# Four gate tiles of the last embedding as Strassen block products

## The chip, the cores and the metric

One Trainium2 chip, one core. The kernel is one launch that runs on that core's engines: TensorE (PE; its weight loads are shown apart as PEld), VectorE (DVE), ScalarE (ACT), GpSimd (POOL) and SyncE (SP, which only issues transfers). The metric is the device time of one execution in microseconds. Before the change it is 1931.98 us, the median of three runs (1931.47 to 1932.03).

## The reference

One inference step of a two-layer decoder: 512 prompt rows and 8 x 4 sample rows, together T = 544 tokens, width 1024. Each layer is a half-weighted SwiGLU, a mixer (a chunked spatial-gating unit in layer 0, forgetting attention in layer 1), a second half-weighted SwiGLU, and a gated embedding of the layer's own input `pe`. What matters here is the end of layer 1:

```python
h = h + 0.5 * swiglu(rmsnorm(h, ffn2_norm[i]), ffn2_w1[i], ffn2_w3[i], ffn2_w2[i])
gate = jax.nn.sigmoid(rmsnorm(h, ple_norm[i]) @ ple_w_gate[i])   # (544, 1024) @ (1024, 1024)
h = h + gate * (pe[i] @ ple_w_proj[i])                            # (544, 256) @ (256, 1024)
```

After layer 1 that `h` is the output y. All arrays are float32.

## The kernel before

**Layout.** The residual `h` lies transposed in SBUF: eight chunks of 128 features, each a row of 544 tokens per partition. A product of two float32 arrays is made from pairs: each operand is split into a rounded half `hi` and a rest `lo` (ACT casts, DVE subtracts: `split_pair` L329/L330 for activations, `_split` L241/L242 for weights, `prep` L341/L342 for a chunk of `h` times its norm's gain), and PE adds hi x hi, hi x lo and lo x hi. A matmul has 128 x 128 weights and 272 of the 544 tokens (HT). A tile of 128 outputs over 1024 features therefore takes 8 x 3 x 2 = 48 matmuls (`mm`, lines L285, L289 and L291 for the three parts). The norm's factor is a number per token, `rstd`; it isn't needed before the product, and multiplies the result.

**Weights.** A list of pieces, in the order of use, is loaded (L208), for some pieces added or subtracted (`_sum`, L227), and split, so many pieces ahead of the product as `ahead` says: (splits, sums, loads), (2, 2, 4) in general and (2, 3, 6) around Strassen products.

**Strassen products.** The wide products of the feed-forward networks (FFN) are made in blocks: 256 features by 256 outputs, against two chunks by two halves of the tokens. Instead of eight block products there are seven (SEVEN = "1562734"), each over sums or differences of blocks. The sums of weight blocks are the pieces with `sum` (`seven`); those of the activations are made by `forms`: for a pair of chunks two ACT copies (L351), three DVE differences (L355, L357, L358) and two splits. One product is 4 x 3 x 2 = 24 matmuls (L538), and adds into one of three PSUM accumulators: A and C are PSUM tiles of the group `ps` (three tiles, rotating), B two tiles of the group `pb`. Behind a step its result is copied or added (L546, L553, L555, L557, L560). A gate then follows in the FFN: times `rstd` (L496), an activation (L499), and so on.

**The last FFN's tail.** The second FFN product is made in parts; its last part runs over chunks 0 to 7 of `h`. Chunk c's PSUM tile is read by `update` (L577), which adds to h[c], and `on_chunk` follows: `prep` for the next norm, and its sum of squares (ACT L368, POOL L370). `next_norm` can also make `forms` behind a chunk (`early`); for the last embedding it makes none. The steps of an FFN stand in a block for which PE, ACT, DVE and POOL keep the order in which the code issues them. Elsewhere a planner orders each engine's instructions, by its own estimate of when each becomes ready.

**The last embedding.** `ple` with layer 1: eight gate tiles by `tile_mm`, each times `rstd` (L765) and through a sigmoid (L766); behind the first two the pieces with w_proj are taken. From the third tile on, a product with `pe` (12 matmuls) follows two tiles behind, is multiplied by the gate (L776), and added to h (L777); then h[n] is stored by SP. Behind gate tile 6 come products 4, 5 and 6, and `ple_last` makes tile 7 in two halves of the tokens, so that the first half's gate, addition and store (L735 to L742) run beside the second half.

Of the kernel before, what the change touches and what calls it, by code (L numbers as in the profile page):

```python
# [36 lines left out]
T = SEQ + NS  # L37
HT = T // 2
# [13 lines left out]
NKP = NC_ // 2  # L52
# [3 lines left out]
SEVEN = "1562734"  # L56
# [16 lines left out]
G_FFN1, G_MIX, G_FFN2, G_PLE = 0, 16, 32, 48  # L73
# [10 lines left out]
COLS = ((0, HT), (HT, T))  # L84
# [3 lines left out]
def woven(x):  # L88

    return x.rearrange("p (a b) -> p b a", a=2)  # L90


def turns(out):

    return out.rearrange("p (b a) -> p b a", a=2)


def unwoven(out):

# [28 lines left out]
def span(p):  # L128

    return p[:].rearrange("p a b -> p (a b)")[:, 512 - HT:512 - HT + T]  # L130


def whole(p):

    return unwoven(span(p))


class Builder:
# [207 lines left out]
    def forms(self, h, gcol, n, xs):  # L346

        nc = self.nc
        x = self.big()
        for a in range(2):  # L350
            nc.scalar.activation(x[:, a, :], h[2 * n + a], AF.Copy, scale=self.gain(gcol + 2 * n + a))  # L351
        t13, t24 = self.tmp(), self.tmp()
        two = lambda t: t.rearrange("p (a b) -> p a b", a=2)
        f13, f24 = self.big(F32R), self.big(F32R)
        nc.vector.tensor_tensor(two(t13), x[:, :, HT:], two(x[:, 0, :]), ALU.subtract)  # L355
        self.split_pair(f13, t13)
        nc.vector.tensor_tensor(t24[:, :HT], x[:, 1, HT:], t13[:, :HT], ALU.subtract)  # L357
        nc.vector.tensor_tensor(t24[:, HT:], x[:, 1, :HT], t24[:, :HT], ALU.subtract)  # L358
        self.split_pair(f24, t24)
        half = lambda t, b: tuple(x[:, b * HT:(b + 1) * HT] for x in t)  # L360
        f13, f24 = ((t[:, 0, :], t[:, 1, :]) for t in (f13, f24))
        return {"1": half(xs[2 * n], 0), "2": half(xs[2 * n + 1], 0), "3": half(xs[2 * n + 1], 1),
                "5": half(f13, 0), "7": half(f13, 1), "6": half(f24, 0), "4": half(f24, 1)}
    def ssq(self, acc, h, cols=slice(0, T), first=False):

        nc = self.nc
        sq = acc[:, cols] if first else self.tmp()[:, cols]
        nc.scalar.activation(sq, h[:, cols], AF.Square)  # L368
        if not first:
            nc.gpsimd.tensor_tensor(acc[:, cols], acc[:, cols], sq, ALU.add)  # L370
# [120 lines left out]
    def gate(self, hid, rstd, j, a, g):  # L491

        nc, tt = self.nc, self.nc.vector.tensor_tensor

        def one():
            tt(g, g, rstd.unsqueeze(1).broadcast_to([P, 2, T]), ALU.mult)  # L496

        def two():
            nc.scalar.activation(g[:, 0], g[:, 0], AF.Silu)  # L499

        def three():
            tt(g[:, 1], g[:, 1], g[:, 0], ALU.mult)  # L502

        def four():
            pair = self.big(F32R)
            self.split_pair(pair, g[:, 1])
            hid[j, a] = pair[:, 0, :], pair[:, 1, :]
        return [one, two, three, four]
# [215 lines left out]
                    if k == n == a == 0:  # L724
                        self.tc.keep_in_program_order(i)

    def ple_last(self, h, gates, rstd, xs, wp, pp, y):

        nc, tt = self.nc, self.nc.vector.tensor_tensor
        c = NC_ - 1  # L730
        a = self.tmp()
        outs = [self.pb(), self.pb()]
        self.cols_mm(outs, self.blocks(self.unit()), xs)
        for (u, v), out in zip(COLS, outs):
            tt(halves(a[:, u:v]), unwoven(out[:, :v - u]), halves(rstd[:, u:v]), ALU.mult)  # L735
            nc.scalar.activation(a[:, u:v], a[:, u:v], AF.Sigmoid)
        outs = [self.ps()[:, 0, :], self.ps()[:, 0, :]]
        self.cols_mm(outs, wp[2 * c:2 * c + 2], pp)
        for (u, v), out in zip(COLS, outs):
            tt(halves(a[:, u:v]), unwoven(out[:, :v - u]), halves(a[:, u:v]), ALU.mult)  # L740
            tt(h[c][:, u:v], h[c][:, u:v], a[:, u:v], ALU.add)
            nc.sync.dma_start(out=y[c][:, u:v], in_=h[c][:, u:v])  # L742

    def ple(self, h, box, layer, on_chunk):
        nc = self.nc
        xs = self.pairs(box)
        pp = []
        for c in range(2):
            raw = self.tmp()
            nc.sync.dma_start(out=raw, in_=self.i["pe"][layer, c])  # L750
            pair = self.big(F32R)
            self.split_pair(pair, raw)
            pp.append((pair[:, 0, :], pair[:, 1, :]))
        rstd, gates, wp = None, [], []
        last = layer == 1
        for c in range(NC_ + 2):
            if c < NC_:
                if rstd is None:
                    p1, rstd = self.tile_rstd(xs, box["acc"])
                else:  # L760
                    p1 = self.tile_mm(xs)

                def gate(p1=p1):
                    a = self.tmp()
                    nc.vector.tensor_tensor(halves(a), whole(p1), halves(rstd), ALU.mult)  # L765
                    nc.scalar.activation(a, a, AF.Sigmoid)  # L766
                    gates.append(a)
                self.evac(gate)
            if c < 2:
                hi, lo = self.unit()  # L770
                wp += [(hi[:, P * k:P * k + P], lo[:, P * k:P * k + P]) for k in range(8)]
            for n in (range(c - 2, c + 1) if last and c == NC_ - 2 else [c - 2] if c >= 2 else ()):
                p2 = self.ps()
                self.mm(p2, wp[2 * n:2 * n + 2], pp, True, True)
                a = gates[n]
                nc.vector.tensor_tensor(halves(a), whole(p2), halves(a), ALU.mult)  # L776
                nc.vector.tensor_tensor(h[n], h[n], a, ALU.add)  # L777
                on_chunk(n)
            if last and c == NC_ - 2:
                self.ple_last(h, gates, rstd, xs, wp, pp, self.o["y"])  # L780
                return


    def square(self, raw):
        sq = self.tmp()
# [584 lines left out]
    def build(self):  # L1370
        nc, i, o = self.nc, self.i, self.o
# [4 lines left out]
                self.add_plain(ap)  # L1376

        def ple_units(n):
            for c in range(NC_):
                self.add_plain(i["wg"][n, c])  # L1380
                if c < 2:
                    self.add_plain(i["wp"][n, c])
# [10 lines left out]
        plain([i["woh"][k, c] for k in range(2) for c in range(NC_ // 2)] + [i["wo"][c] for c in range(NC_)])  # L1393
        self.ffn_pieces(3)
        ple_units(1)

        self.eps = self.const.tile([P, 1], F32, name="eps")
        nc.vector.memset(self.eps, EPS)
# [5 lines left out]
        t = self.pb()  # L1404
# [5 lines left out]
        h = [self.hp[c // 2][:, c % 2, :] for c in range(NC_)]  # L1410
# [15 lines left out]
        box = {"x": {}, "f": [], "acc": self.st()}  # L1426
# [35 lines left out]
        box = nxt  # L1462
        box, rstd = self.kv(h, box, G_FFN1 + 8)
        on, nxt = self.next_norm(h, G_MIX + 8)
        self.ffn(h, box, G_FFN1 + 8, rstd, on)
        box = nxt
        on, nxt = self.next_norm(h, G_FFN2 + 8, early={5: 0, 6: 1})
        self.attention(self.pairs(box), box["acc"], h, on)
        box = nxt
        on, nxt = self.next_norm(h, G_PLE + 8)  # L1470
        self.ffn(h, box, G_FFN2 + 8, None, on)
        box = nxt
        self.ple(h, box, 1, lambda c: nc.sync.dma_start(out=o["y"][c], in_=h[c]))


def _stationary(w):

    k, m = w.shape
    return np.ascontiguousarray(
        w.reshape(k // P, P, m // P, P).transpose(2, 1, 0, 3).reshape(m // P, P, k // P * P))  # L1480


def _blocks(w):

    k, m = w.shape
    return w.reshape(k // 256, 2, P, m // 256, 2, P).transpose(3, 4, 1, 2, 0, 5).reshape(m // 256, 4, P, k // 256, P)


def _constants():
# [30 lines left out]
def _arrays(x_prompt, x_sample, p_prompt, p_sample, cache_k, cache_v, cache_logf, page_table, ffn1_norm, ffn1_w1,  # L1520
# [16 lines left out]
    a["w13q"] = np.stack([_stationary(w[0][:, 256:512]) for w in (ffn1_w1, ffn1_w3)])  # L1537
    a["w13p"], a["w13"], a["w2a"], a["w2b"] = (np.stack(x) for x in (w13p, w13, w2a, w2b))
    a["wg"] = np.stack([_stationary(w) for w in ple_w_gate])
    a["wp"] = np.stack([_stationary(w).reshape(2, 4, P, 2 * P).transpose(0, 2, 1, 3).reshape(2, P, 8 * P)  # L1540
                        for w in ple_w_proj])
    a["win"], a["wout"] = _stationary(gmlp_w_in[0]), _stationary(gmlp_w_out[0])
# [53 lines left out]
```

## Time and profile before

| | |
|---|---|
| median of three runs | 1931.98 us |
| profiled execution, its own time | 1931.48 us |
| its span, first to last instruction | 1929.7 us |
| granted TensorE clock | 1.0 |
| PE busy | 1906.5 us (99%), 16508 matmuls |
| DVE busy | 1457.5 us (76%) |
| ACT busy | 950.2 us (49%) |
| POOL busy | 142.6 us (7%) |
| first gate tile of the last embedding starts | about 1869.6 us |
| DVE ends | 1926.94 us |

A row of the groups reads: line, engine, operation, output <- inputs by the program's names, shapes, count | busy us, mean ns of one | idle time before, with what released it. A row of the timeline reads: start and length in us, engine, line and so on; in brackets is how long the engine was idle before it and for whom. Successive matmuls overlap in the records, so the length of one is not their spacing. A row of the waits gives the waiting instruction, the one it waited for, and the total, the count and the longest.

### The profile page before, as it was taken

To read this page: it belongs to the slowest core of one execution; us is meant where nothing else is said; L and a number is where in the kernel's file an instruction comes from. 1 tells how busy PE (TensorE), PEld (TensorE's weight loads), DVE (VectorE), ACT (ScalarE), POOL (GpSimd) and SP (SyncE) were. 2 spreads that over 40 slices of the span, in tenths; PEclk is the share of its full clock that TensorE was granted. 3 is DMA by queue.
4 is the path that set the end of the run, shared out by engine and by line. 5 is a ranking of instruction groups with operands and counts; after the bars stand their busy time and mean duration, and the time that the engine had idled before them with its cause. 6 is when DMAs were issued, how large, how long until landed. Compare 5 with 4: busy or idle time off the path is not lost.

```text
span 1929.7 us, 39007 instructions
## 1 busy us (share of the span) xinstructions
PE 1906.5 (99%) x16508; PEld 1872.2 (97%) x16508; DVE 1457.5 (76%) x1799; ACT 950.2 (49%) x1396; POOL 142.6 (7%) x190
## 2 busy tenths in 40 slices
PE   9999999999999999999999999999999999999999
PEld 8999999999999999999999999999977899999999
DVE  7887877556788877766578887877476888878774
ACT  7544434424554444454466454444374754444461
POOL 0000000410100000023000000001131300000020
PEclk9999999999999999999999999999999999999999
DMA  5233234312223233431484232324769332332431
GB/s 195 79 112 121 84 123 147 108 48 88 88 88 107 86 120 105 153 104 45 144 306 157 103 129 69 129 86 136 217 210 341 101 110 81 112 113 86 139 109 47
DMA packets 98048, 237.62 MB, mean 123 GB/s; under 512 B 12130, under 2 KB 29826, under 8 KB 97874
## 3 DMA queue, kind: packets, MB, share of 16 engines
q1 hardware_dynamic: 97730, 235.09, 36.9%
q8 instruction: 130, 2.13, 0.5%
q14 instruction: 44, 0.36, 0.1%
q10 hardware_dynamic: 144, 0.04, 0.0%
HBM read 218.65 MB, written 16.44 MB: 122 GB/s over the span
## 4 chain that ended last, share of the span: by engine, by line
PE 89%; DVE 6%; ACT 3%; issue 1%; DMA 1%; POOL 0%; SPq 0%; ACTq 0%; DVEq 0%; POOLq 0%
PE ps L538 31%; PE ps L285 15%; PE ps L291 15%; PE ps L289 15%; PE pb L538 5%; DVE big L242 2%; ACT big L241 1%; DVE big L227 1%; DMA big<-in_cv 1%; PE ps L891 1%; PE ps L892 1%; PE ps L893 1%; DVE big L496 0%; DVE big L330 0%; PE ps L1285 0%
## 5 line engine op out<-in xcount | busy, mean ns | idle before, releaser
L538 PE MATMUL ps<-big,big 128*128 128x272 f32 x5616 | 668.8, 279 | 5.9 <-DVE big L555 3.5
L538 PEld LDWEIGHTS ps<-big,big 128*128 128x128 f32 x5616 | 658.5, 189 | 7.0 <-issue 4.0
L242 DVE TENSOR_TENSOR big<-big,big 128x1024 fp32r<-128x1024 f32 (+2 forms) x505 | 582.8, 1157 | 93.4 <-ACT big L241 92.9
L241 ACT CAST big<-big 128x1024 fp32r<-128x1024 f32 (+2 forms) x505 | 483.1, 977 | 326.5 <-DVE big L227 251.9
L285 PE MATMUL ps<-big,big 128*128 128x272 f32 x2668 | 531.3, 280 | 3.8 <-ACT big L241 2.3
L291 PE MATMUL ps<-big,big 128*128 128x272 f32 x2668 | 529.2, 280 | 1.8 <-DVE big L242 1.7
L289 PE MATMUL ps<-big,big 128*128 128x272 f32 x2668 | 528.3, 279 | 0.0
L285 PEld LDWEIGHTS ps<-big,big 128*128 128x128 f32 x2668 | 408.3, 189 | 8.5 <-ACT big L241 5.7
L291 PEld LDWEIGHTS ps<-big,big 128*128 128x128 f32 x2668 | 407.9, 189 | 3.6 <-DVE big L242 3.1
L289 PEld LDWEIGHTS ps<-big,big 128*128 128x128 f32 x2668 | 407.9, 189 | 0.0
L370 POOL TENSOR_TENSOR st<-st,tmp 128x544 f32<-128x544 f32 (+1 forms) x63 | 87.5, 1389 | 1476.7 <-ACT tmp L368 1476.5
L227 DVE TENSOR_TENSOR big<-big,big 128x1024 f32<-128x1024 f32 x156 | 190.2, 1219 | 0.0
L577 DVE SCALAR_TENSOR_TENSOR big<-ps,big 128x544 f32<-128x544 f32 x128 | 92.5, 723 | 104.0 <-PE ps L291 103.0
L546 ACT COPY tmp<-ps 128x544 f32<-128x544 f32 x117 | 71.6, 612 | 107.5 <-PE ps L538 107.2
L496 DVE TENSOR_TENSOR big<-big,st 128x1088 f32<-128x1088 f32 x88 | 113.2, 1289 | 3.3 <-ACT big L560 2.0
L538 PE MATMUL pb<-big,big 128*128 128x272 f32 x936 | 114.8, 279 | 0.0
L538 PEld LDWEIGHTS pb<-big,big 128*128 128x128 f32 x936 | 111.3, 189 | 0.0
L499 ACT ACTIVATE big<-big 128x544 f32<-128x544 f32 x88 | 58.0, 660 | 88.1 <-DVE big L496 88.0
L341 ACT ACTIVATE big<-big,gains 128x544 fp32r<-128x544 f32 (+1 forms) x80 | 55.3, 703 | 90.3 <-DVE big L577 55.0
L330 DVE TENSOR_TENSOR big<-big,big 128x544 fp32r<-128x544 f32 (+1 forms) x112 | 79.4, 715 | 22.8 <-ACT big L329 22.6
L342 DVE SCALAR_TENSOR_TENSOR big<-big,gains,big 128x544 fp32r<-128x544 f32 (+1 forms) x80 | 64.6, 817 | 23.4 <-ACT big L341 23.4
L329 ACT CAST big<-big 128x544 fp32r<-128x544 f32 (+1 forms) x112 | 71.2, 644 | 11.9 <-DVE big L502 7.5
(218 smaller groups left out, 1388.5 us busy)
## 6 DMA issues: line engine op xcount, KB each, us to landing
big<-in_w SPq DMA_DIRECT2D x156, 512.0 KB
big<-in_w2b SPq DMA_DIRECT2D x96, 384.0 KB
big<-in_w13p SPq DMA_DIRECT2D x16, 512.0 KB
big<-in_w2a SPq DMA_DIRECT2D x16, 512.0 KB
big<-in_win SPq DMA_DIRECT2D x16, 512.0 KB
big<-in_wg SPq DMA_DIRECT2D x16, 512.0 KB
big<-in_ck SPq DMA_DIRECT2D x16, 512.0 KB
big<-in_cv SPq DMA_DIRECT2D x16, 512.0 KB
```

Source lines behind the costliest of these rows:

```text
L227: self.nc.vector.tensor_tensor(t, a, b, ALU.add if op == "+" else ALU.subtract)
L241: self.nc.scalar.copy(hi, src)
L242: self.nc.vector.tensor_tensor(lo, src, hi.bitcast(F32), ALU.subtract)
L285: i = nc.tensor.matmul(o, wh, xh[:, b], start=s, stop=False)
L289: nc.tensor.matmul(o, wh, xl[:, b], start=False, stop=False)
L291: nc.tensor.matmul(o, wl, xh[:, b], start=False, stop=e)
L330: self.nc.vector.tensor_tensor(pair[:, 1, cols], src, pair[:, 0, cols].bitcast(F32), ALU.subtract)
L370: nc.gpsimd.tensor_tensor(acc[:, cols], acc[:, cols], sq, ALU.add)
L496: tt(g, g, rstd.unsqueeze(1).broadcast_to([P, 2, T]), ALU.mult)
L538: nc.tensor.matmul(turns(dst[w]), a[:, c], woven(b), start=k in "152" and kp == 0 and n == 0, stop=kp == NKP - 1 and n == 2, skip_group_ch ...
L546: nc.scalar.copy(t["r" + k], t["C" if k == "5" else "A"])
L577: nc.vector.scalar_tensor_tensor(halves(h[c]), whole(out), 0.5, halves(h[c]), ALU.mult, ALU.add)
```

## The change

Gate tiles 0 to 3 stay as they are. Gate tiles 4 to 7 of layer 1 become seven block products with a new weight array `wg7`, which holds the same weights in blocks. Forms of chunk pairs 0 and 1 are made behind chunks 1 and 3 of the last FFN, those of pairs 2 and 3 behind gate tiles 2 and 3. The order on PE is: gate tiles 0 to 3, products 0 to 3, seven steps, products 4, 6 and 5, and product 7 in two halves. The gates of tiles 4 and 6 come from step "3", those of 5 and 7 from step "4" (each pair is one 1088-wide multiplication by `rstd` and one sigmoid). The additions to h of tiles 4, 6 and 5 run on GpSimd. Reading `pe` becomes a function of its own, with the same instructions.

```diff
+    def strassen(self, xf, done):
+        nc, tt, t = self.nc, self.nc.vector.tensor_tensor, {}
...
+        def step(k):
+            hi, lo = self.unit()
+            self.advance()
+            if k == "2":
+                t["B"] = [self.pb()[:, :HT] for _ in range(2)]
+            elif k in "15":
+                t["A" if k == "1" else "C"] = self.ps()[:, :, :HT]
+            out = t["A" if k in "1674" else "C" if k in "53" else "B"]
+            for kp in range(NKP):
+                xh, xl = xf[kp][k]
+                for n, (a, b) in enumerate(((hi, xh), (hi, xl), (lo, xh))):
+                    for w in range(2):
+                        c = slice(512 * w + P * kp, 512 * w + P * kp + P)
+                        nc.tensor.matmul(turns(out[w] if k == "2" else out[:, w]), a[:, c], woven(b),
...
+            if k in "156":
+                t["r" + k] = self.tmp().rearrange("p (w b) -> p w b", w=2)
+                nc.scalar.copy(t["r" + k], out)
+            elif k == "2":
+                t["g"] = self.big(), self.big()
+                for w in range(2):
+                    tt(halves(t["g"][0][:, w, :HT]), unwoven(out[w]), unwoven(t["r1"][:, w]), ALU.add)
+            elif k == "7":
+                tt(h4(t["g"][1][:, :, HT:]), u4(out), u4(t["r5"]), ALU.add)
+            elif k == "3":
+                tt(h4(t["g"][0][:, :, HT:]), u4(out), u4(t["r6"]), ALU.add)
+                done(0, t["g"][0])
+            else:
+                nc.scalar.copy(h4(t["g"][1][:, :, :HT]), u4(out))
+                done(1, t["g"][1])
...
-    def ple_last(self, h, gates, rstd, xs, wp, pp, y):
+    def ple_last(self, h, box, on_chunk):
...
+        xs, xf, a, wp, rstd = self.pairs(box), box["f"], {}, [], None
+        pp = self.ple_input(1)
+        for c in range(4):
+            if c == 2:
+                self.ahead = (2, 3, 6)
...
+            def gate(c=c, p=p):
+                a[c] = self.tmp()
+                tt(halves(a[c]), whole(p), halves(rstd), ALU.mult)
+                nc.scalar.activation(a[c], a[c], AF.Sigmoid)
+            self.evac(gate)
+            if c >= 2:
+                xf.append(self.forms(h, G_PLE + 8, c, xs))
+            if c < 2:
+                wp += self.blocks(self.unit())
+
+        def product(n):
+            p = self.ps()
+            self.mm(p, wp[2 * n:2 * n + 2], pp, True, True)
+            tt(halves(a[n]), whole(p), halves(a[n]), ALU.mult)
+            (nc.gpsimd.tensor_tensor if n >= 4 else tt)(h[n], h[n], a[n], ALU.add)
+            on_chunk(n)
+
+        def done(k, g):
+            tt(g, g, rstd.unsqueeze(1).broadcast_to([P, 2, T]), ALU.mult)
+            nc.scalar.activation(g, g, AF.Sigmoid)
+            for w in range(2):
+                a[4 + 2 * w + k] = g[:, w]
+        for n in range(4):
+            product(n)
+        step = self.strassen(xf, done)
+        for k in SEVEN:
+            step(k)
+        for n in (4, 6, 5):
+            product(n)
         c = NC_ - 1
-        a = self.tmp()
-        outs = [self.pb(), self.pb()]
-        self.cols_mm(outs, self.blocks(self.unit()), xs)
-        for (u, v), out in zip(COLS, outs):
-            tt(halves(a[:, u:v]), unwoven(out[:, :v - u]), halves(rstd[:, u:v]), ALU.mult)
-            nc.scalar.activation(a[:, u:v], a[:, u:v], AF.Sigmoid)
         outs = [self.ps()[:, 0, :], self.ps()[:, 0, :]]
         self.cols_mm(outs, wp[2 * c:2 * c + 2], pp)
         for (u, v), out in zip(COLS, outs):
...
             nc.sync.dma_start(out=y[c][:, u:v], in_=h[c][:, u:v])
...
         def ple_units(n):
-            for c in range(NC_):
+            for c in range(4 if n else NC_):
                 self.add_plain(i["wg"][n, c])
...
+        d = self.seven([i["wg7"][x] for x in range(4)])
+        self.pieces.extend(d[k] for k in SEVEN)
...
-        on, nxt = self.next_norm(h, G_PLE + 8)
+        on, nxt = self.next_norm(h, G_PLE + 8, early={1: 0, 3: 1})
         self.ffn(h, box, G_FFN2 + 8, None, on)
         box = nxt
-        self.ple(h, box, 1, lambda c: nc.sync.dma_start(out=o["y"][c], in_=h[c]))
+        self.ple_last(h, box, lambda c: nc.sync.dma_start(out=o["y"][c], in_=h[c]))
```

More of the change, by code (lines that the diff above doesn't have):

```diff
@@ L363, in forms @@
                 "5": half(f13, 0), "7": half(f13, 1), "6": half(f24, 0), "4": half(f24, 1)}
+    def strassen(self, xf, done):
+        nc, tt, t = self.nc, self.nc.vector.tensor_tensor, {}
+        u4 = lambda t: t.rearrange("p w (b a) -> p w a b", a=2)
+        h4 = lambda t: t.rearrange("p w (a b) -> p w a b", a=2)
+        def step(k):
[12 more added lines that the diff above has]
+                        nc.tensor.matmul(turns(out[w] if k == "2" else out[:, w]), a[:, c], woven(b),
+                                         start=k in "152" and kp == 0 and n == 0, stop=kp == NKP - 1 and n == 2,
+                                         skip_group_check=True)
+            if k in "156":
[13 more added lines that the diff above has]
+                done(1, t["g"][1])
+        return step
     def ssq(self, acc, h, cols=slice(0, T), first=False):
@@ L725, in cols_mm @@
                         self.tc.keep_in_program_order(i)
-    def ple_last(self, h, gates, rstd, xs, wp, pp, y):
-        nc, tt = self.nc, self.nc.vector.tensor_tensor
-        c = NC_ - 1
-        a = self.tmp()
-        outs = [self.pb(), self.pb()]
-        self.cols_mm(outs, self.blocks(self.unit()), xs)
-        for (u, v), out in zip(COLS, outs):
-            tt(halves(a[:, u:v]), unwoven(out[:, :v - u]), halves(rstd[:, u:v]), ALU.mult)
-            nc.scalar.activation(a[:, u:v], a[:, u:v], AF.Sigmoid)
+    def ple_last(self, h, box, on_chunk):
+        nc, tt, y = self.nc, self.nc.vector.tensor_tensor, self.o["y"]
+        xs, xf, a, wp, rstd = self.pairs(box), box["f"], {}, [], None
[3 more added lines that the diff above has]
+                self.ahead = (2, 3, 6)
+            if rstd is None:
+                p, rstd = self.tile_rstd(xs, box["acc"])
+            else:
+                p = self.tile_mm(xs)
+            def gate(c=c, p=p):
[25 more added lines that the diff above has]
+            product(n)
+        c = NC_ - 1
         outs = [self.ps()[:, 0, :], self.ps()[:, 0, :]]
@@ L739, in ple_last, with ple_input @@
         for (u, v), out in zip(COLS, outs):
-            tt(halves(a[:, u:v]), unwoven(out[:, :v - u]), halves(a[:, u:v]), ALU.mult)
-            tt(h[c][:, u:v], h[c][:, u:v], a[:, u:v], ALU.add)
+            tt(halves(a[c][:, u:v]), unwoven(out[:, :v - u]), halves(a[c][:, u:v]), ALU.mult)
+            tt(h[c][:, u:v], h[c][:, u:v], a[c][:, u:v], ALU.add)
             nc.sync.dma_start(out=y[c][:, u:v], in_=h[c][:, u:v])
+    def ple_input(self, layer):
+        pp = []
+        for c in range(2):
+            raw = self.tmp()
+            self.nc.sync.dma_start(out=raw, in_=self.i["pe"][layer, c])
+            pair = self.big(F32R)
+            self.split_pair(pair, raw)
+            pp.append((pair[:, 0, :], pair[:, 1, :]))
+        return pp
     def ple(self, h, box, layer, on_chunk):
@@ L746, in ple @@
         xs = self.pairs(box)
[L747 to L753, printed above, removed]
+        pp = self.ple_input(layer)
         rstd, gates, wp = None, [], []
-        last = layer == 1
         for c in range(NC_ + 2):
@@ L771, in ple @@
                 wp += [(hi[:, P * k:P * k + P], lo[:, P * k:P * k + P]) for k in range(8)]
-            for n in (range(c - 2, c + 1) if last and c == NC_ - 2 else [c - 2] if c >= 2 else ()):
+            for n in [c - 2] if c >= 2 else ():
                 p2 = self.ps()
@@ L778, in ple @@
                 on_chunk(n)
-            if last and c == NC_ - 2:
-                self.ple_last(h, gates, rstd, xs, wp, pp, self.o["y"])
-                return
     def square(self, raw):
@@ L1486, in _blocks, with _pairs @@
     return w.reshape(k // 256, 2, P, m // 256, 2, P).transpose(3, 4, 1, 2, 0, 5).reshape(m // 256, 4, P, k // 256, P)
+def _pairs(w):
+    h = w.shape[1] // 2
+    return np.stack([_blocks(w[:, :h]), _blocks(w[:, h:])], 3).reshape(4, P, 1024)
 def _constants():
@@ L1539, in _arrays @@
     a["wg"] = np.stack([_stationary(w) for w in ple_w_gate])
+    a["wg7"] = _pairs(ple_w_gate[1][:, D // 2:])
     a["wp"] = np.stack([_stationary(w).reshape(2, 4, P, 2 * P).transpose(0, 2, 1, 3).reshape(2, P, 8 * P)
```

## The prediction

> **What bounds the kernel now.** I read the page first: busy times, granted clock, and the costliest groups.
>
> ```profile
> PE 1906.5 (99%) x16508; PEld 1872.2 (97%) x16508; DVE 1457.5 (76%) x1799; ACT 950.2 (49%) x1396; POOL 142.6 (7%) x190
> ...
> PEclk9999999999999999999999999999999999999999
> ```
>
> TensorE (PE) works for 1906.5 of 1929.7 us at the full granted clock, so the time is the number of matmuls times their spacing, plus what little PE waits. The spacing is in the chain that ended last, in order of time (start, us, engine, tile, line, count), and the same view shows how the program ends:
>
> ```profile
> 1825.24 2.78 PE pb L538 x24
> ...
> 1918.84 5.56 PE pb L722 x48
> 1924.40 0.71 PE ps L722 x6
> ...
> 1925.20 0.45 DVE tmp L740
> ...
> 1926.50 0.44 DVE big L741
> ```
>
> One Strassen product (24 matmuls) takes 2.78 us, one direct gate tile (48) takes 5.56: 0.116 us per matmul in either form. At the end six more matmuls of L722 follow the x6, so PE ends at 1924.40 + 12 x 0.116 = 1925.8; VectorE (DVE) ends at 1926.94, 1.1 later, and the last store closes the span at 1929.7, 2.8 later still. Busy time by stretch of the last embedding shows what room DVE has:
>
> ```profile
> 1877.00:1885.00 8.00, 8.00 (x72) 8.00 (x71) 7.60 (x10) 5.77 (x7) 0.00 (x0) 1.00 0.00 0
> 1885.00:1900.00 15.00, 15.00 (x132) 15.00 (x131) 6.25 (x9) 3.79 (x5) 0.00 (x0) 1.00 0.10 38
> 1900.00:1910.00 10.00, 10.00 (x89) 10.00 (x88) 3.65 (x6) 1.31 (x2) 0.00 (x0) 1.00 0.08 29
> ```
>
> The columns after the length are PE, weight load, DVE, ScalarE (ACT), GpSimd (POOL). PE is never idle here. DVE is full until 1885 and then two thirds idle. So the change can gain only by fewer matmuls, and loses wherever it makes PE wait or lengthens the 1.1 + 2.8 us behind PE's end.
>
> **1. Matmuls removed.** Four direct gate tiles are 4 x 48 = 192; seven block products are 7 x 24 = 168. The gain is 24 x 0.116 = **2.78 us**, 0.14% of the time. That is the whole of it: a measurement of this kernel can tell about 0.2% (3.9 us) from no change, so even the full gain lies inside that. The products with wp (12 matmuls each) keep their number, the weight bytes too (four blocks of 512 KB for four tiles).
>
> **2. Forms behind chunks 1 and 3 of the last FFN.** This is the step I worked longest on. The FFN's tail lies in the block whose order is written out by hand, so DVE and ACT run it strictly as issued: for chunk c the update L577 (it reads the PSUM tile and frees it), the split of a weight, `prep` L341/L342, the square L368, and now the forms. The rows of the tail, DVE first:
>
> ```profile
> 1848.38 0.72 DVE L577 SCALAR_TENSOR_TENSOR big<-ps,big 128x544 f32<-128x544 f32 x1
> ...
> 1850.61 0.72 DVE L577 SCALAR_TENSOR_TENSOR big<-ps,big 128x544 f32<-128x544 f32 x1
> 1851.25 1.48 DVE L242 TENSOR_TENSOR big<-big,big 128x768 fp32r<-128x768 f32 x1
> ...
> 1853.34 0.71 DVE L577 SCALAR_TENSOR_TENSOR big<-ps,big 128x544 f32<-128x544 f32 x1
> ...
> 1857.25 0.72 DVE L577 SCALAR_TENSOR_TENSOR big<-ps,big 128x544 f32<-128x544 f32 x1 [1.11 <-PE ps L291]
> ...
> 1865.59 0.72 DVE L577 SCALAR_TENSOR_TENSOR big<-ps,big 128x544 f32<-128x544 f32 x1 [1.62 <-PE ps L291]
> ...
> 1869.76 0.72 DVE L577 SCALAR_TENSOR_TENSOR big<-ps,big 128x544 f32<-128x544 f32 x1 [1.62 <-PE ps L291]
> ```
>
> ```profile
> 1849.78 0.65 ACT L368 ACTIVATE tmp<-big 128x544 f32<-128x544 f32 x1
> ```
>
> These are the updates of chunks 1, 2, 3, 4, 6 and 7; chunks from 4 on come every 4.17 us, and the one of chunk 4 waited 1.11 us for PE, so only from there has DVE slack. What one set of forms costs stands where the gMLP makes one behind a chunk:
>
> ```profile
> 475.01 1.38 ACT L351 ACTIVATE big<-big,gains 128x544 f32<-128x544 f32 x2
> 476.42 0.75 DVE L355 TENSOR_TENSOR tmp<-big 128x544 f32<-128x544 f32 x1 [1.04 <-ACT big L351]
> 477.21 0.44 DVE L357 TENSOR_TENSOR tmp<-big,tmp 128x272 f32<-128x272 f32 x1
> 477.26 0.65 ACT L329 CAST big<-tmp 128x544 fp32r<-128x544 f32 x1 [0.87 <-DVE tmp L355]
> 477.68 0.44 DVE L358 TENSOR_TENSOR tmp<-big,tmp 128x272 f32<-128x272 f32 x1
> 478.04 0.72 DVE L330 TENSOR_TENSOR big<-tmp,big 128x544 fp32r<-128x544 f32 x1
> ...
> 478.68 0.72 DVE L714 TENSOR_TENSOR big<-ps,big 128x544 f32<-128x544 f32 x1
> ```
>
> There the planner fills the waits: L357 and L358 run during the cast, and an update (L714) between the two subtractions L330. In the hand-written order nothing may pass: two copies, L355, cast, L330, L357, L358, cast, L330, each waiting for the one before: 1.38 + 0.75 + 0.65 + 0.72 + 0.44 + 0.44 + 0.65 + 0.72 = 5.75, about 5.9 with the hand-overs. The first set starts when ACT has issued the square of chunk 1, about 1850.3, so DVE comes to the update of chunk 2 at 1856.2 instead of 1850.61. Two updates in a row without a wait stand 2.2 us apart (1848.38 to 1850.61), so chunk 3 follows at 1858.5; its square ends near 1860.5, the second set takes 5.9, and chunk 4's update starts at 1866.4 and frees its tile at 1867.1. Three PSUM tiles rotate: chunk 7 takes the tile of chunk 4, and PE wants it when chunk 6 is done, 0.2 before 1865.59. PE then waits **1.8 us**. Chunk 2's own tile is wanted by chunk 5 at 1857.05 and is free at 1856.9. Bounds: 0 if the order turned out not to bind, 2.8 if two DVE/POOL collisions of 0.5 (L242 above at 1.48 beside a free one of 0.96, below) fall into it. I take 1.8, since each row is from this stage or of the same shapes.
>
> **3. The late DVE and the embedding.** Chunk 7's update then comes at about 1874 instead of 1869.76; the first gate tile reads chunk 7 last, 4.9 us after its start near 1871.4, and its pair is ready at about 1876: covered, barely. `rstd` arrives some 14 us after the first gate tile starts, as now (L392 below ends at 1883.4, the tile started at 1869.56). Costs from the groups:
>
> ```profile
> 1882.66 0.72 DVE L392 SCALAR_TENSOR_TENSOR st<-tmp,st 128x544 f32<-128x544 f32 x1
> ```
>
> ```profile
> L242 DVE TENSOR_TENSOR big<-big,big 128x1024 fp32r<-128x1024 f32 (+2 forms) x505 | 582.8, 1157 | 93.4 <-ACT big L241 92.9
> L227 DVE TENSOR_TENSOR big<-big,big 128x1024 f32<-128x1024 f32 x156 | 190.2, 1219 | 0.0
> L777 DVE TENSOR_TENSOR big<-big,tmp 128x544 f32<-128x544 f32 x15 | 10.9, 725 | 0.5
> L776 DVE TENSOR_TENSOR tmp<-ps,tmp 128x544 f32<-128x544 f32 x15 | 10.8, 723 | 7.7 <-PE ps L291 7.0 <-ACT tmp L766 0.7
> ```
>
> Gates 0 to 3 and products 0 to 3 end 4 x 5.56 + 0.46 (four matmuls for the norm's sums) + 4 x 1.39 = 28.3 us after that start, so DVE has about 14 us for: four gate evictions and eight operations of products at 0.72 (8.7), two sets of forms at 3.1 of DVE time (6.1), two splits and two sums (4.8): 19.6. It falls 5.6 short. But PE needs only product 0's multiplication for product 3, product 1's for step 1, product 2's for step 5; the adds and the last multiplications, some 5 us, can run under the steps, where PE has 19.5 us and DVE about 12 of its own. I put the wait at **0.7**, between 0 and 1.6. The nearest rows for a Strassen start that follows forms agree in size: four FFNs together waited
>
> ```profile
> PE ps L538 <- DVE big L555: 3.5, 3, 2.1
> ...
> PE ps L538 <- ACT tmp L546: 2.4, 3, 1.3
> ```
>
> 5.9 us, 1.5 each. Those also had the hidden activations to make.
>
> **4. The end.** Count from the end of step 4. Rows of the same shapes:
>
> ```profile
> L496 DVE TENSOR_TENSOR big<-big,st 128x1088 f32<-128x1088 f32 x88 | 113.2, 1289 | 3.3 <-ACT big L560 2.0
> ...
> L499 ACT ACTIVATE big<-big 128x544 f32<-128x544 f32 x88 | 58.0, 660 | 88.1 <-DVE big L496 88.0
> ...
> L560 ACT COPY big<-ps 128x544 f32<-128x544 f32 x39 | 23.9, 613 | 76.5 <-PE ps L538 76.5
> ```
>
> ACT finishes the sigmoid of step 3's pair at about +0.5 (1088 wide, between one and two of 0.66), copies step 4's tile until 1.1, DVE scales until 2.4, then multiplies product 4 (until 3.1) and 6 (3.8); the second sigmoid is done by 3.6, product 5 by 5.0. PE runs the four products until 5.56 unhindered, as before. But additions 4, 6 and 5 go to POOL:
>
> ```profile
> 1852.81 1.82 POOL L370 TENSOR_TENSOR st<-st,tmp 128x544 f32<-128x544 f32 x1 [0.90 <-ACT tmp L368]
> ```
>
> ```profile
> 1838.33 0.96 DVE L242 TENSOR_TENSOR big<-big,big 128x768 fp32r<-128x768 f32 x1
> ...
> 1853.97 1.47 DVE L242 TENSOR_TENSOR big<-big,big 128x768 fp32r<-128x768 f32 x1
> ```
>
> A POOL add of this shape takes 1.4 to 1.8, one after the other: 3.2 to 4.6, to 6.0, to 7.5. DVE alone would end at 6.7 (PE's end plus 1.1). So the last POOL add ends 0.8 after it, and it stores a whole 272 KB tile behind it. And L242 lost 0.5 us, ending 0.8 us after the POOL add did: DVE's two adds of product 7 may be held the same way, to about 8.2. SP issues the stores, and the queue passes them in order:
>
> ```profile
> L742 SPq DMA_DIRECT2D out_y<-big x2: 332/332/332, 1926.1 to 1927.0; - x2
> ```
>
> If tile 5's store stands ahead of product 7's two, those wait for the third POOL add (7.5) and then 0.33 each, which still ends with the held adds. That is **1.3 us** later, bounds 0 (POOL starts earlier than I think) and 1.9 (three adds at 1.8 less overlap).
>
> [...]
>
> **Sum.** -2.78 + 1.8 + 0.7 + 1.3 = +1.0 us. The profiled execution took 1931.48 (1.78 around its span), so 1932.5; the median of the runs shown is 0.5 above it: 1932.98, which I call **1933.0**, between 1931.3 (-0.7: 1.3 + 0 + 0.8 of waits) and 1935.3 (+3.3, a little under all upper bounds).
>
> **Rivals.**
> All extra work is hidden and the end is as now: -2.78, **1929.2**. For it: DVE's free two thirds after 1885, no PE wait there. Against: the strict order in the FFN's tail, and POOL's three serial adds.
> Slower: DVE becomes the bound at the start of the steps. If the forms and splits are queued ahead of the multiplications that free PSUM tiles, the 5.6 us of shortage can't run under the steps and PE waits for all of it: -2.78 + 1.8 + 5.6 + 1.3 = +5.9, **1937.9**. It decides from the point where more than some 3.6 us of it falls before step 5. For it: DVE leaves the FFN 4 us later than now and was already full until 1885. Against: the planner orders this stage and let an update pass a form in the gMLP rows.
> The change isn't confined: the planner orders the whole program again and shifts work elsewhere, several us in either direction, **1927 or 1937**; nothing in the code before the last FFN changes, so little speaks for it.
>
> **Chances.** Forecast 0.64; full gain 0.17; DVE-bound start 0.12; order elsewhere 0.07 (0.04 faster, 0.01 no change, 0.02 slower). Faster by over 0.2%: 0.04; within: 0.82; slower: 0.14. The range takes in the full gain and the edge of the slower cases: 1929.0 to 1936.2.
>
> **What would show it.** Step 1: L538's successor with 168 matmuls, no L285 group of four gate tiles. Step 2: the update of chunk 2 near 1856 and of chunk 4 near 1866, with a PE wait on L577 before chunk 7; if PE runs through, the step is wrong. Step 3: a PE wait on a multiplication at product 3 or step 1; none, or over 3 us, is wrong. Step 4: POOL's third add ending after DVE's last but one, and a last add of DVE far over 0.44 us. A time under 1930 means that the waits were hidden, one over 1936 that DVE bounds a stage.

## The result and the profile after

The changed kernel takes 1934.57 us (median of 22 runs, 1933.52 to 1935.82) against 1931.28 us of the kernel before, run beside it: the ratio is 1.0017, 95% interval 1.0012 to 1.0023. That is 3.3 us more, inside the 0.2% that the prediction called no change, and resolved by the many runs. The profiled execution took 1934.36 us, its span is 1932.6 us, 2.9 longer than before.

The busy times of the page after the change:

```profile
PE 1904.2 (99%) x16484; PEld 1868.8 (97%) x16484; DVE 1478.2 (76%) x1824; ACT 963.6 (50%) x1416; POOL 147.7 (8%) x193
```

24 matmuls are gone, and PE's busy time fell by 2.3 us. The waits of PE from 1750 us on, where before there were none (waiting line, line waited for, total us, times, longest):

```profile
PE ps L285 <- DVE big L616: 1.9, 1, 1.9
PE ps L285 <- ACT big L341: 0.4, 1, 0.4
PE ps L289 <- DVE big L342: 0.3, 1, 0.3
```

L616 is `update` (L577 before). The timeline shows where these waits stand; columns as before, rows of DVE and PE in order of time:

```profile
1848.12 0.72 DVE L616 SCALAR_TENSOR_TENSOR big<-ps,big 128x544 f32<-128x544 f32 x1
...
1855.85 0.72 DVE L616 SCALAR_TENSOR_TENSOR big<-ps,big 128x544 f32<-128x544 f32 x1
...
1864.90 0.40 PE L291 MATMUL ps<-big,big 128*128 128x272 f32 x2
...
1866.37 0.72 DVE L616 SCALAR_TENSOR_TENSOR big<-ps,big 128x544 f32<-128x544 f32 x1
...
1867.23 0.47 PE L285 MATMUL ps<-big,big 128*128 128x272 f32 x2 [1.93 <-DVE big L616]
...
1869.46 1.74 DVE L242 TENSOR_TENSOR big<-big,big 128x1024 fp32r<-128x1024 f32 x1
1871.12 1.86 DVE L342 SCALAR_TENSOR_TENSOR big<-big,gains,big 128x544 fp32r<-128x544 f32 x1
...
1876.11 0.40 PE L291 MATMUL ps<-big,big 128*128 128x272 f32 x2
1876.90 0.79 DVE L342 SCALAR_TENSOR_TENSOR big<-big,gains,big 128x544 fp32r<-128x544 f32 x1 [0.82 <-ACT big L341]
1876.92 0.50 PE L285 MATMUL ps<-big,big 128*128 128x272 f32 x2 [0.42 <-ACT big L341]
1877.74 0.50 PE L289 MATMUL ps<-big,big 128*128 128x272 f32 x2 [0.32 <-DVE big L342]
```

The updates of chunks 1, 2 and 4 begin at 1848.12, 1855.85 and 1866.37. PE issues two matmuls at 1864.90 and could go on at 1865.13; it goes on at 1867.23, when chunk 4's update has freed the tile. At 1876.11 it comes to chunk 7 in the first gate tile, and waits once for the rounded half of that chunk's pair and once for the rest. Starts of matmuls tell more than the waits, because the first matmuls behind a wait are also spaced a little wider (the two at 1867.23 take 0.31 us to the next pair, otherwise 0.23): added up over all starts from 1836 us on, what lies above 0.116 us is 2.2 us at chunk 7, 1.3 in the first gate tile and 0.3 where gate tile 3 begins, 3.8 us in all, against 0.0 before. I call this sum **the gaps**.

The end, from the timeline:

```profile
1920.05 1.29 DVE L797 TENSOR_TENSOR big<-big,st 128x1088 f32<-128x1088 f32 x1
...
1922.58 0.73 DVE L792 TENSOR_TENSOR big<-ps,big 128x544 f32<-128x544 f32 x1 [1.24 <-ACT big L798]
...
1923.21 1.28 DVE L797 TENSOR_TENSOR big<-big,st 128x1088 f32<-128x1088 f32 x1
...
1923.38 4.92 POOL L793 TENSOR_TENSOR big<-big,big 128x544 f32<-128x544 f32 x3 [44.48 <-DVE big L792]
...
1924.99 1.55 PE L761 MATMUL ps<-big,big 128*128 128x272 f32 x12
...
1926.31 0.78 DVE L812 TENSOR_TENSOR big<-ps,big 128x272 f32<-128x272 f32 x2
1927.01 1.95 DVE L813 TENSOR_TENSOR big<-big,big 128x272 f32<-128x272 f32 x2
1928.63 0.33 SPq L814 DMA_DIRECT2D out_y<-big  x1
1929.06 0.38 SPq L1547 DMA_DIRECT2D out_y<-big  x1
1929.53 0.40 SPq L814 DMA_DIRECT2D out_y<-big  x1
```

PE ends at 1924.99 + 1.55 = 1926.5, DVE at 1928.96, and the last store is issued at 1929.53. The two additions of product 7 (L813) take 1.95 us together, where the two of before took 0.44 each. One at a time, they are

```profile
1927.01 1.60 DVE L813 TENSOR_TENSOR big<-big,big 128x272 f32<-128x272 f32 x1
...
1928.53 0.43 DVE L813 TENSOR_TENSOR big<-big,big 128x272 f32<-128x272 f32 x1
```

so only the first was held. The store of tile 5 (L1547) stands between product 7's two. From VectorE's end the last store is issued 0.6 us later and the span ends 3.1 us after that; before the change these were 0.0 and 2.7 us. From PE's end to the span's end it is 6.1 us, 3.9 before. I call this **the end**.

That accounts for the difference: 24 matmuls -2.8, gaps +3.8, end +2.2, and this execution came to the FFN's tail 0.25 earlier (chunk 0's update at 1845.88, before at 1846.13): +2.9 us of span.

### The profile page after: what moved, and what is told of

It is laid out like the page before. It is cut to its first block, busy times and chain, and to the rows that moved or that the text cites. A ratio compares the mean times of both kernels' runs of the same rounds, so it can differ in the third digit from the quotient of the medians.

```text
span 1932.6 us, 39005 instructions
## 1 busy us (share of the span) xinstructions
PE 1904.2 (99%) x16484; PEld 1868.8 (97%) x16484; DVE 1478.2 (76%) x1824; ACT 963.6 (50%) x1416; POOL 147.7 (8%) x193
## 4 chain that ended last, share of the span: by engine, by line
PE 85%; DVE 7%; ACT 3%; DMA 2%; issue 2%; SPq 0%; POOL 0%; DVEq 0%; ACTq 0%
PE ps L577 31%; PE ps L285 14%; PE ps L291 14%; PE ps L289 14%; PE pb L577 5%; DVE big L242 2%; ACT big L241 1%; DVE big L227 1%; PE ps L963 1%; PE ps L964 1%; PE ps L965 1%; PE ps L383 1%; DVE big L330 1%; DMA tmp<-rows 1%; DVE big L535 0%
## 5 line engine op out<-in xcount | busy, mean ns | idle before, releaser
L577 PE MATMUL ps<-big,big 128*128 128x272 f32 x5616 | 668.8, 279 | 5.9 <-DVE big L594 3.5
L577 PEld LDWEIGHTS ps<-big,big 128*128 128x128 f32 x5616 | 658.5, 189 | 7.0 <-issue 4.0
L242 DVE TENSOR_TENSOR big<-big,big 128x1024 fp32r<-128x1024 f32 (+2 forms) x508 | 586.0, 1156 | 95.1 <-ACT big L241 94.3
L241 ACT CAST big<-big 128x1024 fp32r<-128x1024 f32 (+2 forms) x508 | 485.5, 975 | 330.1 <-DVE big L227 256.4
L285 PE MATMUL ps<-big,big 128*128 128x272 f32 x2620 | 521.5, 280 | 5.7 <-DVE big L616 3.3
L291 PE MATMUL ps<-big,big 128*128 128x272 f32 x2620 | 519.4, 280 | 2.1 <-DVE big L242 1.7
L289 PE MATMUL ps<-big,big 128*128 128x272 f32 x2620 | 518.5, 279 | 0.3 <-DVE big L342 0.3
L285 PEld LDWEIGHTS ps<-big,big 128*128 128x128 f32 x2620 | 400.3, 189 | 10.9 <-ACT big L241 7.2
L291 PEld LDWEIGHTS ps<-big,big 128*128 128x128 f32 x2620 | 400.0, 189 | 4.2 <-DVE big L242 3.8
L289 PEld LDWEIGHTS ps<-big,big 128*128 128x128 f32 x2620 | 400.4, 189 | 0.5 <-DVE big L342 0.5
L227 DVE TENSOR_TENSOR big<-big,big 128x1024 f32<-128x1024 f32 x160 | 195.0, 1219 | 0.0
L616 DVE SCALAR_TENSOR_TENSOR big<-ps,big 128x544 f32<-128x544 f32 x128 | 92.4, 722 | 98.2 <-PE ps L291 97.2
L577 PE MATMUL pb<-big,big 128*128 128x272 f32 x936 | 114.8, 279 | 0.0
L577 PEld LDWEIGHTS pb<-big,big 128*128 128x128 f32 x936 | 111.3, 189 | 0.0
L342 DVE SCALAR_TENSOR_TENSOR big<-big,gains,big 128x544 fp32r<-128x544 f32 (+1 forms) x80 | 65.7, 830 | 23.9 <-ACT big L341 23.9
```

The source lines that it names most:

```text
L227: self.nc.vector.tensor_tensor(t, a, b, ALU.add if op == "+" else ALU.subtract)
L241: self.nc.scalar.copy(hi, src)
L242: self.nc.vector.tensor_tensor(lo, src, hi.bitcast(F32), ALU.subtract)
L285: i = nc.tensor.matmul(o, wh, xh[:, b], start=s, stop=False)
L289: nc.tensor.matmul(o, wh, xl[:, b], start=False, stop=False)
L291: nc.tensor.matmul(o, wl, xh[:, b], start=False, stop=e)
```

## The experiments

Theory A: the forms in the hand-written order hold back the updates, and PE waits for it. Theory D: GpSimd's additions and VectorE's instructions hold each other up at the end, as a split beside one of GpSimd's took 1.47 us instead of 0.96 before the change, and the last store waits for both. The rivals stand in the expectations. All runs are timed beside the kernel before. The profiled executions reach the FFN's tail up to 3.3 us apart (chunk 0's update starts between 1844.90 and 1848.21). So I compare "the stretch", from chunk 0's update in the last FFN to the span's end (83.5 us before the change, 86.7 after), beside the ratio. The ratio is of medians of many executions; stretch, gaps and end come from one profiled execution of each kernel.

| run | ratio to before (95%) | stretch, us | gaps, us | end, us |
|---|---|---|---|---|
| before | | 83.5 | 0.0 | 3.9 |
| the change | 1.0017 (1.0012 to 1.0023) | 86.7 | 3.8 | 6.1 |
| forms only, unused | 1.0025 (1.0016 to 1.0034) | 88.0 | 4.5 | 3.9 |
| all forms in the embedding | 1.0026 (1.0016 to 1.0036) | 88.5 | 5.5 | 6.1 |
| forms reordered | 1.0005 (0.9996 to 1.0015) | 83.9 | 1.0 | 6.1 |
| additions on VectorE | 1.0012 (1.0003 to 1.0021) | 86.1 | 4.1 | 5.2 |
| reordered, VectorE | 0.9999 (0.9990 to 1.0008) | 83.3 | 1.3 | 5.2 |
| and gates by tile | 0.9999 (0.9990 to 1.0008) | 83.3 | 1.2 | 5.2 |
| gates by tile, GpSimd | 1.0007 (0.9998 to 1.0016) | 84.5 | 1.7 | 5.8 |
| and product 4 first | 0.9996 (0.9987 to 1.0005) | 82.7 | 1.0 | 4.8 |
| and one set early | 1.0005 (0.9996 to 1.0014) | 84.5 | 2.6 | 5.0 |

In each row the stretch is 83.5 (less 2.8 where the matmuls are gone), plus the gaps, plus the end less 3.9, within 0.1 us: nothing else moved.

**Forms only.** In the kernel before:

```diff
-        on, nxt = self.next_norm(h, G_PLE + 8)
+        on, nxt = self.next_norm(h, G_PLE + 8, early={1: 0, 3: 1})
```

> The kernel before, with the two sets of forms behind chunks 1 and 3 of the last FFN made and never used; everything else as before. Theory A (the hand-written order of the FFN's tail holds back the updates behind the forms): PE waits about 2.1 us at chunk 7 for chunk 4's PSUM tile and about 1.2 us in the first gate tile for chunk 7's pair, so the span grows by 3.3 us (2.8 to 4.0). Rival B (the forms lie beside other work, and what the change lost it lost in the embedding itself): no new PE wait, span within 0.5 us of before.

Measured: 1.0025, gaps of 4.5 us. Theory A holds, and the size is larger than expected for a reason that I hadn't thought of. The timeline's row at chunk 7:

```profile
1867.08 0.47 PE L285 MATMUL ps<-big,big 128*128 128x272 f32 x2 [1.92 <-DVE big L577]
```

and busy time by stretch (columns as in the prediction; the granted clock is the third number from the right):

```profile
1868.60:1871.90 3.30, 3.30 (x17) 3.30 (x16) 3.30 (x4) 2.83 (x4) 2.39 (x2) 0.51 0.81 258
```

In the changed kernel the same stretch reads

```profile
1868.70:1872.00 3.30, 3.30 (x31) 3.30 (x30) 3.30 (x4) 2.88 (x4) 2.40 (x2) 1.00 0.79 288
```

The wait is the same (2.1 us above the usual spacing). But behind it, in this execution, TensorE ran 3.3 us at half its clock, and 17 matmuls overlap that window instead of 31. The 1.7 us that this cost also hid the second wait: PE came to chunk 7's pair after it was ready. So the forms alone lose 2.2 us at the PSUM tile, and the 1.2 us of the second wait didn't show as such here. The remaining 0.7 us of the gaps is a wait that ends at 1890.73, for the PSUM tile that gate 0's multiplication (L765) frees.

**All forms in the embedding.** In the changed kernel:

```diff
-        on, nxt = self.next_norm(h, G_PLE + 8, early={1: 0, 3: 1})
+        on, nxt = self.next_norm(h, G_PLE + 8)
...
-            if c >= 2:
-                xf.append(self.forms(h, G_PLE + 8, c, xs))
+            xf.append(self.forms(h, G_PLE + 8, c, xs))
```

> The changed kernel with the forms of pairs 0 and 1 made behind gate tiles 0 and 1 of the embedding, outside the hand-written order. Theory A: the 2.1 and 1.2 us of PE waits in and behind the FFN's tail are gone; DVE has 6.1 us more to do before the steps but comes to the embedding some 4 us earlier, so PE waits 0 to 2.5 us there; 1.0 to 3.3 us faster than the changed kernel, most likely 2.5. Rival B: within 0.5 us of the changed kernel. Rival C (the embedding has no room for two more sets): slower than the changed kernel by 1 us or more, with PE waits at products 0 to 3 or at the first two steps.

Measured: 1.0026. The waits in the FFN's tail are gone, as theory A says, but rival C decides: PE waits elsewhere, from 1860 us on

```profile
PE ps L285 <- ACT big L241: 2.0, 2, 1.5
PE ps L383 <- DVE big L242: 0.9, 2, 0.5
PE ps L291 <- DVE big L242: 0.5, 1, 0.5
PE ps L383 <- ACT big L241: 0.2, 1, 0.2
```

All are waits for splits of weights (L241, L242), at gate tiles 2 and 3 and at the steps: the planner put forms ahead of them. In the planner's order the embedding has no room for four sets. Two sets in the FFN cost less, and the next run shows that most of what they cost was their order.

**Forms reordered.** For the first two sets (the others stay as they were), the differences come first and a cast runs beside them:

```diff
         nc.vector.tensor_tensor(two(t13), x[:, :, HT:], two(x[:, 0, :]), ALU.subtract)
-        self.split_pair(f13, t13)
+        nc.scalar.copy(f13[:, 0], t13)
         nc.vector.tensor_tensor(t24[:, :HT], x[:, 1, HT:], t13[:, :HT], ALU.subtract)
         nc.vector.tensor_tensor(t24[:, HT:], x[:, 1, :HT], t24[:, :HT], ALU.subtract)
-        self.split_pair(f24, t24)
+        nc.scalar.copy(f24[:, 0], t24)
+        nc.vector.tensor_tensor(f13[:, 1], t13, f13[:, 0].bitcast(F32), ALU.subtract)
+        nc.vector.tensor_tensor(f24[:, 1], t24, f24[:, 0].bitcast(F32), ALU.subtract)
```

> The changed kernel with the same forms at the same places, but in another issue order within the first two sets: the three differences first, then the two casts on ScalarE, then the two subtractions, so that one cast runs beside the differences. Theory A: a set holds DVE 4.6 instead of 5.9 us, chunk 2's update comes 1.3 and chunk 4's 2.6 us earlier, and both PE waits (2.1 and 1.2 us) shrink to under 0.3 us in all: about 3 us faster than the changed kernel, 0.2 to 0.5 faster than before. Rival B: within 0.5 us of the changed kernel.

Measured: 1.0005, 2.8 us less in the stretch than the change. The updates of chunks 2 and 4 (L625 in this kernel):

```profile
1854.59 0.72 DVE L625 SCALAR_TENSOR_TENSOR big<-ps,big 128x544 f32<-128x544 f32 x1
...
1863.78 0.72 DVE L625 SCALAR_TENSOR_TENSOR big<-ps,big 128x544 f32<-128x544 f32 x1
```

1.3 and 2.6 us earlier than in the change, as expected, and the wait at chunk 7 is gone. In the first gate tile 0.9 of 1.3 us stay, where I had expected both waits together under 0.3: without the wait at chunk 7 PE also comes to this tile 2.2 us sooner, and chunk 7's pair is ready only 2.6 us sooner, measured from chunk 0's update. This is the strongest evidence for theory A: the same instructions at the same places, and three quarters of the gaps go with their order alone.

**Additions on VectorE.**

```diff
-            (nc.gpsimd.tensor_tensor if n >= 4 else tt)(h[n], h[n], a[n], ALU.add)
+            tt(h[n], h[n], a[n], ALU.add)
```

> The changed kernel with the additions to h of tiles 4, 6 and 5 on VectorE instead of GpSimd. Theory D (GpSimd's three additions and VectorE's two-input instructions exclude each other, and the last store waits for both): VectorE has 3 x 0.64 us more of its own, but nothing waits 1.3 us for GpSimd; the end of the span comes 5.0 to 5.5 us behind PE's end instead of 6.1, so 0.5 to 1.0 us faster than the changed kernel. Rival E (VectorE bounds the end, and GpSimd takes work from it): 0.5 to 2 us slower than the changed kernel.

Measured: 1.0012, and the end is 5.2 us: PE's last row and DVE's last are

```profile
1927.35 1.79 PE L761 MATMUL ps<-big,big 128*128 128x272 f32 x12
...
1930.63 0.78 DVE L813 TENSOR_TENSOR big<-big,big 128x272 f32<-128x272 f32 x2
```

The span of this execution is 1934.3, so 5.2 behind PE's end at 1929.1. As theory D says, GpSimd's additions lengthen the end: with three more additions of its own VectorE ends no later behind PE (2.3 us instead of 2.4), product 7's two take 0.78 instead of 1.95, and no store of another tile stands between its own. But of the 0.9 us only 0.1 is VectorE's. The other 0.7 lies in the stores: the last one is issued 0.1 instead of 0.6 us behind VectorE's end, and the span ends 2.8 instead of 3.1 us after that.

**Both edits.** 

> The changed kernel with both edits: the first two sets of forms in the other issue order, and the additions of tiles 4, 6 and 5 on VectorE. If the two losses (PE waits behind the hand-written order; GpSimd's additions at the end) are separate, their effects add: no PE wait at chunk 7, about 1.0 us of PE gaps left, PE's end to the span's end 5.2 us instead of 6.1: matmuls -2.8, gaps +1.0, end +1.2 against before, so -0.6 us (between -1.5 and +0.5) against before. Rival (VectorE is one shared limit, and what one edit frees the other uses up): no better than the better of the two alone, +0.5 to +1.5 us against before.

Measured: 0.9999, stretch 83.3, 0.2 less than before (0.6 expected). The effects add: 86.7 less 2.8 less 0.6 is 83.3. The gain of the matmuls is still used up, by 1.3 us of gaps and an end 1.3 longer.

**Gates by tile.**

```diff
-            tt(g, g, rstd.unsqueeze(1).broadcast_to([P, 2, T]), ALU.mult)
-            nc.scalar.activation(g, g, AF.Sigmoid)
             for w in range(2):
+                tt(g[:, w], g[:, w], rstd, ALU.mult)
+                nc.scalar.activation(g[:, w], g[:, w], AF.Sigmoid)
                 a[4 + 2 * w + k] = g[:, w]
```

> As the run with both edits, and the gates of tiles 4 and 6 and of 5 and 7 made tile by tile (two 544-wide multiplications and sigmoids for each 1088-wide one). Theory F (what is left of the longer end is VectorE idling 1.2 us for the wide sigmoid before product 4, in front of a queue that it then works off in a row): the wait shrinks to under 0.3 us, PE's end to the span's end falls from 5.2 to 4.2 us (3.9 before the change), 0.8 to 1.2 us faster than with both edits alone, about -1.6 against before. Rival G (VectorE's total work behind the last step is the limit): within 0.3 us of the run with both edits.

Measured: 0.9999, no different. The wait in front of product 4's multiplication, with both edits and then with gates by tile (L801 in both):

```profile
1921.26 0.72 DVE L801 TENSOR_TENSOR big<-ps,big 128x544 f32<-128x544 f32 x1 [1.24 <-ACT big L807]
```

```profile
1920.43 0.72 DVE L801 TENSOR_TENSOR big<-ps,big 128x544 f32<-128x544 f32 x1 [1.08 <-PE ps L291]
```

Theory F falls as it stood: the sigmoid was early enough now, but product 4 itself wasn't done. The planner had spread its first matmuls among the last steps and put its last two behind step 4. The size is what rival G expects; whether VectorE's work is the limit whatever its start is tried two runs below.

**Gates by tile, GpSimd.** The same with the additions on GpSimd again.

> As the run with the gates tile by tile, but with the additions of tiles 4, 6 and 5 on GpSimd as in the change. Theory D (exclusion between GpSimd's additions and VectorE's two-input instructions): the additions start about a microsecond earlier, but still exclude the scaling of the second pair and the additions of product 7: the end takes 0.5 to 1.0 us longer than with VectorE's additions. Rival H (only the late start of the additions mattered): as short an end as with VectorE's additions, or shorter.

Measured: 1.0007, stretch 84.5, 1.2 us longer than on VectorE: end 5.8 instead of 5.2, and 0.7 instead of 0.2 us of a gap at PE's last six matmuls, which waited for a PSUM tile that a late VectorE held. The scaling of the second pair runs beside the first addition and is stretched (two instructions that take 1.35 together in the run before this one):

```profile
1920.26 2.50 DVE L807 TENSOR_TENSOR big<-big,st 128x544 f32<-128x544 f32 x2
```

GpSimd's first addition runs beside them, from 1920.42 to 1922.17, as theory D has it. The longer end is again in the stores: VectorE ends as soon behind PE as with its own additions (2.3 us), but the last store, now tile 5's, is issued 0.5 instead of 0.1 us behind VectorE's end, and the span ends 3.1 instead of 2.8 us after that. Rival H is not put to the test: behind the end of step 4 the first addition starts at 1.1 us, in the change at 1.2, not a microsecond earlier.

**Product 4 first.** Gates by tile, additions on VectorE, and

```diff
         for k in SEVEN:
+            if k == "4":
+                product(4)
             step(k)
-        for n in (4, 6, 5):
+        for n in (6, 5):
             product(n)
```

> As the run with gates tile by tile and all additions on VectorE, and product 4 issued in front of step 4 instead of behind it. If the wait of 1.1 us that was left there came from where the planner had put product 4's matmuls, VectorE multiplies product 4 about 1 us earlier against step 4's end, and PE's end to the span's end falls from 5.2 to 4.7 (4.4 to 4.9): 0.3 to 0.6 us faster than that run. Rival (VectorE's work behind step 4 is the limit whatever its start): 5.1 or more.

Measured: 0.9996 (0.9987 to 1.0005), the shortest stretch of all, 82.7: 0.6 less than without it, 0.8 less than before. VectorE multiplies product 4 from 0.8 us in front of step 4's end instead of 0.3 behind it, and the end is 4.8, as expected. The median is 1930.12 against 1931.28 beside it, but the interval holds 1. No version was shown to beat the kernel before.

**One set early.** As the last, with `early={1: 0}` and pair 1's set behind gate tile 1.

> As the run with product 4 first, but only the set of pair 0 is made in the hand-written order (behind chunk 1); the set of pair 1 is made behind gate tile 1. If the PE gaps of 0.9 us in the first gate tile come from VectorE's lateness after the second set, they vanish, and what shows is whether the embedding has room for one set more: with room, 0.5 to 0.9 us faster than the run with product 4 first; without (the weight splits queue behind the forms, as with all four sets there), PE gaps of 1 to 3 us at gate tiles 2 and 3 or the first steps, 0.5 to 2 us slower than it.

Measured: 1.0005. The waits of the first gate tile vanish, as they should if they came from the second set, but from 1860 us on PE waits

```profile
PE ps L285 <- ACT big L241: 0.9, 1, 0.9
PE ps L392 <- DVE tmp L801: 0.7, 1, 0.7
```

at gate tile 3 for a weight's split and at step 1 (L392) for product 1's multiplication, 1.8 us more stretch in all. In the planner's order the embedding has no room even for a third set.

## Why the prediction was right or wrong

The forecast was no change that a measurement can tell, +1.0 us; measured are +3.3 us (ratio) and +2.9 us (spans), inside the range. But the sum held only a third of that. In the stretch, which grew by 3.2, the missing 2.2 us are 1.3 at chunk 7's pair, which the sum had at nothing, 0.9 at the end and 0.4 at chunk 7, less 0.4 in the embedding.

**Matmuls removed**: right, 24 of them and 2.8 us, and all experiments add up with that number.

**Forms in the hand-written order**: right, with its mechanism and place. Predicted were updates at 1856.2 (chunk 2) and 1866.4 (chunk 4) and a PE wait of 1.8 us in front of chunk 7; measured are 1855.85, 1866.37 and 2.2 us. That the second figure fits to 0.03 us is partly luck: chunks 2 and 3 came 0.4 us earlier than I had them, and 0.5 us in the second set's first difference took it back. It lies beside an addition of GpSimd (1860.28 to 1862.11), a collision that I had taken only into the upper bound; in the first set it takes 0.75:

```profile
1861.45 1.24 DVE L355 TENSOR_TENSOR tmp<-big 128x544 f32<-128x544 f32 x1 [0.55 <-ACT big L351]
```

The reordering removed PE's wait with nothing else changed.

**Chunk 7's pair "covered, barely"**: wrong. I had its pair ready at about 1876, against a need at 1876.3. It was ready at 1877.7, and PE lost 1.3 us. The step that failed is the pricing of VectorE behind the second set: I took a collision with GpSimd's sums of squares only into the upper bound, and between the updates of chunks 5 and 6 there were two, a split of 1.74 (1.22 free) and L342 of 1.86 (0.78 free): 1.6 us. In the kernel before, where VectorE isn't late, such collisions (the splits of 1.48 and 1.47) cost PE nothing. The set of pair 1 is what makes it late: with only pair 0's there, this wait was absent.

**The late VectorE and the embedding**: 0.7 predicted, 0.3 measured, and not where I put it: PE waited at gate tile 3 for the PSUM tile of gate 0, since `rstd` was late, not at the products, where the sign that I had set for this step asked for it. The shortage of VectorE did run under the steps, as argued; how near it was to its limit the two runs with more sets there show: 2.6 us of gaps in the embedding with three sets and 5.5 with four, against 0.1 to 0.4 at gate tile 3 with two.

**The end**: 1.3 predicted, 2.2 measured; VectorE's part was right and the stores' part was not. Behind PE's end VectorE ended at 1.16 us before the change and at 2.41 after, 1.25 later, where the sum had 1.3. That difference held although each time was off: behind the end of step 4 PE ended at 4.4 us instead of 5.6, since the planner pulled product 4's matmuls among the steps, GpSimd at 6.2 instead of 7.5, and VectorE at 6.8 instead of 8.2. The step that failed is the queue of stores, which I had put at nothing ("which still ends with the held adds"). Tile 5's store, whose addition ended at 1928.31, went out at 1929.06, between product 7's two (1928.63 and 1929.53), and from VectorE's end to the span's end it took 3.6 us instead of the 2.7 of before. With the additions on VectorE it took 2.9. So of the 2.2 us, 0.9 go when the additions move to VectorE, most of it in the stores; why the span ends 0.3 us sooner behind the last store then is not shown. Another 0.4 go when product 4 gets a place of its own (end 4.8 instead of 5.2); the remaining 0.9 are mostly VectorE's work, which still ends 0.8 us later behind PE than before the change.

Beside GpSimd's additions the scalings by `rstd` and the additions of product 7 stretched (with gates by tile 2.50 us for two scalings that take 1.35 otherwise, in the change 1.95 for two additions of 0.44); the multiplications from PSUM did not (0.72 to 0.73). In the change the scaling at 1923.21 took its usual 1.28, and GpSimd's addition, which began 0.17 us behind it, took 2.33, where the other two took 1.35 and 1.33.

**The rivals.** The full gain didn't come for the two reasons named against it. The slower case (VectorE the bound at the steps' start) did not occur here but did with four sets in the embedding, at 5.5 us of gaps, through late weight splits rather than late multiplications; that it was priced at 5.6 is chance, since that price was for two sets there. Nothing shows that an order elsewhere changed the time: in every run the difference of the medians agrees with that of the stretches within 0.7 us.

## What to carry to other kernels

PE was the bound here and busy throughout, and the gain of the removed matmuls was known beforehand (24 x 0.116 = 2.8 us). In such a case spend the working on where the replacement's work stands in each queue: here an order that was written out by hand turned 3 us of VectorE work into 6 us of occupied queue, and moving one subtraction of each set behind the other differences gave back 2.8 us. Work given to another engine wasn't free here: beside an addition on GpSimd, VectorE's own took 1.60 us instead of 0.43, and with those additions on VectorE itself, VectorE ended no later (2.3 us behind PE instead of 2.4). And price the stores behind the last result too: with one of another tile between the last two, it took 0.9 us more from VectorE's end to the span's end (3.6 instead of 2.7).

## What the runs showed of the hardware that I had not expected

In the run with forms only, a PE wait of 2.1 us was followed by 3.4 us at half the clock, which cost another 1.7 us. In the changed kernel, and in the one with the additions on VectorE, a wait of the same length at the same place was followed by none: the granted clock from 1840 to 1925 us was 1.00 in both, 0.98 in the run with forms only. PE in the same two stretches of 3.41 us in the run with forms only, then in the change (columns: stretch, its length, PE busy and matmuls, granted clock, DMA share, GB/s):

```profile
1864.98:1868.39 3.41, 1.49 (x13) 1.00 0.63 167
1868.39:1871.80 3.41, 3.41 (x17) 0.50 0.77 240
```

```profile
1864.98:1868.39 3.41, 1.48 (x13) 1.00 0.01 2
1868.39:1871.80 3.41, 3.41 (x32) 1.00 0.71 253
```

In both the first stretch holds the whole wait, and PE is busy for 1.49 and 1.48 us of it. Behind it the granted clock is 0.50 in the one execution and 1.00 in the other. So the wait's length and PE's busy time around it don't part the two cases; what does, these rows don't show, and no run set a wait's length on purpose.
